# Score matmuls of the two heads of a pair issued alternately, in a two-layer hybrid attention trunk

## The chip, the cores and the metric

The kernel runs on one core of one Trainium2 chip. The metric is the time of one execution on the device, in microseconds (us); lower is better. The time before is 905.24 us, the median of 3 runs.

## What is computed

Two layers work on 256 tokens of width 1024, in float32. In each layer, the normalized input goes through one projection that gives q, k and v for 24 heads of 64 features and three gates. Twelve heads use softmax over dilated windows (three groups of four heads, mixed by their softmax sums), six use softmax with a block gate (at 256 tokens it is plain causal softmax, "MoBA"), and six use stick-breaking. The outputs are projected, gated, summed, projected again and added to the input; a squared-ReLU MLP follows. Shortened:

```python
for layer in range(2):
    h = rmsnorm(x, norm_mix)
    q, k, v, gates = split(h @ w_in)           # q and k of 18 heads with partial rotary
    o_a = dilated_mixture(q_a, k_a, v_a)       # 12 heads in 3 groups
    o_b = causal_softmax(q_b, k_b, v_b)        # 6 heads
    o_c = stick_breaking(q_c, k_c, v_c)        # 6 heads
    x = x + (g0 * (o_a @ wa) + g1 * (o_b @ wb) + g2 * (o_c @ wc)) @ w_o
    h = rmsnorm(x, norm_mlp)
    x = x + square(relu(h @ w_up)) @ w_down
out = rmsnorm(x, norm_final)
```

## The kernel before

All activations stay on the chip; 280 pieces of weights (128 x 1024 float32, 140 per layer) stream in from memory. Each piece is split into a high and a low part, `wh` on ACT (L115) and `wl` on DVE (L116), and a projection is three matmuls per 128 x 128 of weights: low part times high part of the input (L195), high times high (L196), high times low (L197), each with 256 columns.

In the first stage of a layer `MIX_ORDER` sets the order of the projections: v, then q and k of a pair of heads (`qk_pair`), then gates. After a pair's q and k the attention work that has become possible is put into the list `units`, and after each projection `run_units` takes one or two functions from its front. So attention work stands between projections. Behind that a scheduler orders the instructions of each engine by priority and by when their inputs should be there; what it made of the program is the order in which PE and the others execute.

One pair of heads shares a tile of q and k: head 0 lies on partitions 0 to 63, head 1 on 64 to 127. A score matmul contracts over 64 features and so uses only half of the array's rows: `scores` (L280) for softmax, `scores_t` (L284) for stick-breaking. They are plain float32, and each is recorded in the trace as two weight loads and two matmuls; the projections, in a rounded float32 format, are recorded as one of each.

- `att_softmax` with three groups (the dilated heads, twice per layer): its function `score` makes four units of scores, one after the other: head 0 and head 1 for the first 128 queries (3 x 128 columns each, in the two halves of the PSUM tile `s0`, a bank each), then head 0 and head 1 for the other queries (3 x 256 columns, a PSUM tile `s1` of two banks per head). After each comes `softmax_rows`: DVE adds the mask and finds the extreme (L311), ACT takes exp (L313), DVE normalizes (L315, L319).
- `att_softmax` with one group (MoBA, three times per layer): one PSUM tile, a bank per head, with 256 and 128 columns each.
- `att_c` (stick-breaking, three times per layer): `logs` writes the scores of both heads to one PSUM tile, a bank per head, and works them over with ACT, DVE, POOL and matmuls by a triangle (L415 to L418).
- `values` transposes the softmax rows on PE (L364 to L366) and multiplies with v (L306, L307).

PSUM tiles of the tag `s` have two buffers, shared by all of these. The scores of a head were written as

```python
for j in range(2):
    for g in range(3):
        scores(s0[:, j, g * P:(g + 1) * P], fs[g], j, T0, T0)
    softmax_rows(...)
```

Of the kernel before, what the change touches and what calls it, by code (L numbers as in the profile page):

```python
# [15 lines left out]
P = 128  # L16
D = 1024
KT = D // P
S = 256
# [39 lines left out]
def trunk(ctx: ExitStack, tc: tile.TileContext, w, x, norms, gfin, consts, out):  # L59
# [21 lines left out]
    def s_bank():  # L81
        return PS("s", [P, 2, 512], 2)
# [3 lines left out]

# [1 line left out]
    raw = {}  # L88
# [63 lines left out]
    def norm_split(hl, nrm, d):  # L152
        """high and low parts of x * g for one tile of features"""
        g = cst["norms"][:, nrm, d:d + 1]
        act.activation(hl[:, 0, d], xres[:, d], AF.Copy, scale=g)
        dve.scalar_tensor_tensor(hl[:, 1, d], xres[:, d], g, hl[:, 0, d].bitcast(F32),
                                 op0=ALU.mult, op1=ALU.subtract)

    def sumsq(d, acc):
        """acc += x*x over the tiles of features"""  # L160
        if d == 0:
            act.activation(acc, xres[:, d], AF.Square)
        else:
            sq = T("sq", [P, S], 3)
            act.activation(sq, xres[:, d], AF.Square)  # L165
            pool.tensor_tensor(acc, acc, sq, op=ALU.add)  # L166

    def rms_cols(acc):
        """[128, 2]: the factor of each token"""
        p = t_bank()  # L170
        for h in range(2):
            pe.matmul(p[:, h:h + 1], acc[:, h * P:(h + 1) * P], ones[:, 0:1], start=True, stop=True)
        r = T("rc", [P, 2], 8)
        dve.tensor_scalar(r, p[:, 0:2], 1.0 / D, EPS, op0=ALU.mult, op1=ALU.add)
        rc = T("rc", [P, 2], 8)
        pool.tensor_tensor(rc, r, mhalf, op=ALU.pow)
        return rc

    def bcast(rc):
        """PSUM [128, 256]: the factor of each token on every partition"""  # L180
        dg = T("sq", [P, 2, P], 3)
        for h in range(2):
            dve.tensor_scalar(dg[:, h], ident, rc[:, h:h + 1], None, op0=ALU.mult)
        p = t_bank()
        pe.matmul(p[:, 0:S], ones, dg.rearrange("p a b -> p (a b)"), start=True, stop=True)
        return p[:, 0:S]

    def proj(dst, n, hl, nk=KT, first=True, last=True, koff=0, woff=0):
        """dst[128 features, 256] (+)= W piece^T X"""
        hi, lo = split(n)  # L190
        for k in range(nk):
            c = (woff + k) * P
            a = (first and k == 0)
            z = (last and k == nk - 1)
            pe.matmul(dst, lo[:, c:c + P], hl[:, 0, koff + k], start=a, stop=False, skip_group_check=True)  # L195
            pe.matmul(dst, hi[:, c:c + P], hl[:, 0, koff + k], start=False, stop=False, skip_group_check=True)  # L196
            pe.matmul(dst, hi[:, c:c + P], hl[:, 1, koff + k], start=False, stop=z, skip_group_check=True)  # L197
# [12 lines left out]
    for layer in range(DEPTH):  # L210
# [9 lines left out]
        def normalized():  # L220
            """high and low parts of x * g * r"""
            for d in range(KT):
# [5 lines left out]

# [1 line left out]
        V = {}  # L230
# [26 lines left out]

# [1 line left out]
        QK = {}  # L259
# [30 lines left out]
        def o_head(po, oF, j):  # L290
            """o^T of a head: the parts from the high and the low part of v are added"""
            tmp = T("tmp", [DH, S], 2)
            act.activation(tmp, po[DH:P, 0:S], AF.Copy)
            dve.tensor_tensor(oF[j * DH:(j + 1) * DH], po[0:DH, 0:S], tmp, op=ALU.add)
# [5 lines left out]
        def pv_mm(po, head, kt, ph, pl, first, last):  # L300
            """po[v high and low, q] += v^T p^T"""
            c, s = divmod(head, 8)
# [18 lines left out]
        def att_softmax(fs, kt_out, units):  # L321
            """two heads (one pair) over the union of the keys of the groups fs"""
            G = len(fs)
            p0 = {}
            p1 = {}
            mA = cst["maskA"] if G == 3 else cst["maskB"].unsqueeze(1)

            def score():
                den = T("den", [P, 4], 3)
                if G == 3:  # L330
                    s0 = s_bank()
                    t0 = T("wk", [P, 2, 3, P], WK)
                    for j in range(2):
                        for g in range(3):
                            scores(s0[:, j, g * P:(g + 1) * P], fs[g], j, T0, T0)
                        softmax_rows(t0[:, j], s0[:, j, 0:384].rearrange("p (a b) -> p a b", a=3),
                                     mA[:, :, T1], den[:, j:j + 1])
                        p0[j] = t0[:, j]
                    for j in range(2):
                        s1 = s_bank()  # L340
                        t1 = T("wk", [P, 3, S], WK)
                        sf = s1.rearrange("p a b -> p (a b)")
                        for g in range(3):
                            scores(sf[:, g * S:(g + 1) * S], fs[g], j, T1, TT)
                        softmax_rows(t1, sf[:, 0:768].rearrange("p (a b) -> p a b", a=3), mA, den[:, 2 + j:3 + j])
                        p1[j] = t1
                else:
                    s1 = s_bank()
                    t1 = T("wk", [P, 2, 384], WK)
                    for j in range(2):  # L350
                        scores(s1[:, j, 0:S], fs[0], j, T1, TT)
                        scores(s1[:, j, S:384], fs[0], j, T0, T0)
                        softmax_rows(t1[:, j, 0:S], s1[:, j, 0:S], cst["maskB"], den[:, j:j + 1])
                        softmax_rows(t1[:, j, S:384], s1[:, j, S:384], cst["maskB"][:, T1], den[:, 2 + j:3 + j])
                        p1[j] = t1[:, j:j + 1, 0:S]
                        p0[j] = t1[:, j:j + 1, S:384]

# [19 lines left out]

            units += [score, lambda: values(0), lambda: values(1)]

        def att_c(i, units):  # L380
# [13 lines left out]
            def strict(x):  # L394
                """zero where the key isn't before the query"""
                for y in diag(x):
# [3 lines left out]
            def logs():  # L400
                st = s_bank()
                for j in range(2):
                    scores_t(st[:, j, 0:S], f, j, TT, T0, True)
                    scores_t(st[:, j, S:384], f, j, T1, T1, False)
                z = st[:, :, 0:384]
# [66 lines left out]

# [1 line left out]
        mg = hilo_slot()  # L474
# [14 lines left out]

# [1 line left out]
        acc = T("acc", [P, S], 1)  # L491
# [11 lines left out]

# [1 line left out]
        n = base + 76  # L505
# [228 lines left out]
```

## Time and profile before

| | |
|---|---|
| Median of 3 runs | 905.24 us (905.21 to 905.29) |
| Profiled execution, span from first to last instruction | 903.7 us |
| PE matmul busy | 891.9 us (99%), 6672 matmuls |
| DVE, ACT, POOL busy | 602.0, 493.8, 56.5 us (67%, 55%, 6%) |
| Granted TensorE clock | 0.9 or more of full speed in all 40 slices |
| Memory traffic | 151.5 MB, mean 168 GB/s |

The median lies 1.5 us above the span of the profiled execution. A matmul's recorded duration overlaps the next one's, so a busy PE does not mean that nothing is to be gained; what a matmul costs is read from the distance between the starts of neighbouring matmuls. The chain of waits is followed back from the last instruction and tells which engine's work the end hangs on.

### The profile page before, as it was taken

The page shows a single profiled execution, that of the slowest core. Times are in us where ns is not written, and L with a number is a line of the kernel's source. Part 1 is how long each engine was busy: PE and PEld are TensorE (multiplying, and loading weights), DVE is VectorE, ACT ScalarE, POOL GpSimd, SP SyncE. Part 2 cuts the span into 40 slices and gives each one's busy share as a digit, 9 for nine tenths or more (in the row PEclk, how much of TensorE's full clock was granted, in tenths as well). Part 3 has the DMA queues.
Part 4 walks back from the last instruction along what each step waited for, and adds up shares of the span by engine and source line. Part 5 has one row for each costly group of instructions (what it writes and reads, how often), then busy time and mean ns, then how long its engine had stood idle before and what let it go on. Part 6 is the DMA issues. An engine that isn't in the chain of part 4 may idle for free.

```text
span 903.7 us, 16383 instructions
## 1 busy us (share of the span) xinstructions
PE 891.9 (99%) x6672; PEld 846.8 (94%) x6672; DVE 602.0 (67%) x899; ACT 493.8 (55%) x724; POOL 56.5 (6%) x72
## 2 busy tenths in 40 slices
PE   8999999999999999999999999999999999999997
PEld 6899999999999999999988999999999999999995
DVE  6887777764986555555588868688558865555554
ACT  5655555667464444444466565656573654444442
POOL 7000100000020000000020101000000300000000
PEclk9999999999999999999999999999999999999999
DMA  8764434444656666666556544344456656566541
GB/s 301 234 189 136 142 118 139 128 153 156 182 157 201 193 182 181 182 182 184 164 186 188 171 134 139 119 140 123 157 164 187 187 171 201 187 186 188 185 140 46
DMA packets 43562, 151.47 MB, mean 168 GB/s; under 512 B 4960, under 2 KB 6368, under 8 KB 43488
## 3 DMA queue, kind: packets, MB, share of 16 engines
q1 hardware_dynamic: 43056, 149.90, 53.0%
q8 instruction: 52, 0.85, 0.4%
q10 hardware_dynamic: 432, 0.54, 0.2%
q14 instruction: 22, 0.18, 0.1%
HBM read 149.37 MB, written 1.05 MB: 166 GB/s over the span
## 4 chain that ended last, share of the span: by engine, by line
PE 91%; DVE 5%; DMA 2%; issue 1%; ACT 0%; SPq 0%; POOL 0%; POOLq 0%; DVEq 0%; ACTq 0%
PE mm L195 18%; PE mm L196 17%; PE mm L197 17%; PE s L546 3%; PE s L548 3%; PE s L547 3%; PE s L280 3%; PE s L572 3%; PE s L573 3%; PE s L574 3%; DVE wl L116 2%; DMA raw<-in_w_dram 2%; PE s L197 2%; PE s L196 2%; PE s L195 2%
## 5 line engine op out<-in xcount | busy, mean ns | idle before, releaser
L116 DVE TENSOR_TENSOR wl<-raw,wh 128x1024 fp32r<-128x1024 f32 (+1 forms) x282 | 345.1, 1226 | 227.1 <-ACT wh L115 226.9
L115 ACT ACTIVATE wh<-raw 128x1024 fp32r<-128x1024 f32 (+1 forms) x282 | 295.8, 1053 | 305.7 <-PE mm L197 175.5
L195 PE MATMUL mm<-hl,wl 128*128 128x256 f32 x1344 | 383.2, 285 | 1.7 <-DVE xres L496 1.7
L196 PE MATMUL mm<-hl,wh 128*128 128x256 f32 x1344 | 382.6, 285 | 0.0
L197 PE MATMUL mm<-hl,wh 128*128 128x256 f32 x1344 | 380.3, 284 | 0.2 <-DVE hl L227 0.2
L195 PEld LDWEIGHTS mm<-hl,wl 128*128 128x128 f32 x1344 | 256.9, 191 | 6.6 <-issue 2.7
L196 PEld LDWEIGHTS mm<-hl,wh 128*128 128x128 f32 x1344 | 257.0, 191 | 3.8 <-issue 2.0
L197 PEld LDWEIGHTS mm<-hl,wh 128*128 128x128 f32 x1344 | 256.3, 191 | 0.8 <-DVE hl L227 0.4
L546 PE MATMUL s<-ga,wl 128*128 128x256 f32 x256 | 72.5, 284 | 0.0
L547 PE MATMUL s<-ga,wh 128*128 128x256 f32 x256 | 72.3, 283 | 0.0
L548 PE MATMUL s<-ga,wh 128*128 128x256 f32 x256 | 72.2, 283 | 0.0
L572 PE MATMUL s<-wl,ga 128*128 128x512 f32 x128 | 50.1, 391 | 0.0
L573 PE MATMUL s<-wh,ga 128*128 128x512 f32 x128 | 50.0, 391 | 0.0
L546 PEld LDWEIGHTS s<-ga,wl 128*128 128x128 f32 x256 | 49.1, 192 | 0.5 <-DVE sq L633 0.2
L574 PE MATMUL s<-wh,ga 128*128 128x512 f32 x128 | 49.5, 389 | 0.0
L547 PEld LDWEIGHTS s<-ga,wh 128*128 128x128 f32 x256 | 49.1, 192 | 0.1
L548 PEld LDWEIGHTS s<-ga,wh 128*128 128x128 f32 x256 | 49.0, 192 | 0.2 <-DVE ga L535 0.2
L166 POOL TENSOR_TENSOR acc<-acc,sq 128x256 f32<-128x256 f32 x21 | 19.6, 934 | 414.0 <-ACT sq L165 239.6
L195 PE MATMUL s<-hl,wl 128*128 128x256 f32 x128 | 36.2, 283 | 0.0
L196 PE MATMUL s<-hl,wh 128*128 128x256 f32 x128 | 36.2, 283 | 0.0
L197 PE MATMUL s<-hl,wh 128*128 128x256 f32 x128 | 36.2, 283 | 0.0
L280 PE MATMUL s<-qk 64*128 64x128 f32 (+1 forms) x144 | 32.0, 347 | 0.0
(139 smaller groups left out, 1162.3 us busy)
## 6 DMA issues: line engine op xcount, KB each, us to landing
raw<-in_w_dram SPq DMA_DIRECT2D x278, 512.0 KB, 4.2
raw<-in_w_dram SPq DMA_DIRECT2D x4, 256.0 KB, 4.3
xres<-in_x_dram SPq DMA_DIRECT2D x8, 128.0 KB, 5.6
wk<-in_gfin_dram SPq DMA_DIRECT2D x2, 256.0 KB, 4.3
out_dram<-V SPq DMA_DIRECT2D x2, 256.0 KB, 2.3
out_dram<-V ACTq DMA_DIRECT2D x2, 256.0 KB, 2.2
c_maskA<-in_maskA_dram SPq DMA_DIRECT2D x1, 384.0 KB, 6.1
c_rope<-in_rope_dram SPq DMA_DIRECT2D x1, 256.0 KB, 5.6
```

Source lines behind the costliest of these rows:

```text
L115: act.activation(hi[:, c:c + step], r[:, c:c + step], AF.Copy)
L116: dve.tensor_tensor(lo[:, c:c + step], r[:, c:c + step], hi[:, c:c + step].bitcast(F32), op=ALU.subtract)
L195: pe.matmul(dst, lo[:, c:c + P], hl[:, 0, koff + k], start=a, stop=False, skip_group_check=True)
L196: pe.matmul(dst, hi[:, c:c + P], hl[:, 0, koff + k], start=False, stop=False, skip_group_check=True)
L197: pe.matmul(dst, hi[:, c:c + P], hl[:, 1, koff + k], start=False, stop=z, skip_group_check=True)
L280: pe.matmul(dst, t[own, 0, qs], t[own, 1, ks], start=True, stop=True, skip_group_check=True)
L546: pe.matmul(dst, lo[:, c], uh[:, j % 2], start=a, stop=False, skip_group_check=True)
L547: pe.matmul(dst, hi[:, c], uh[:, j % 2], start=False, stop=False, skip_group_check=True)
L548: pe.matmul(dst, hi[:, c], ul[:, j % 2], start=False, stop=z, skip_group_check=True)
L572: pe.matmul(dst, uh[:, j % 2, k], lo[:, c], start=j == 0, stop=False)
L573: pe.matmul(dst, uh[:, j % 2, k], hi[:, c], start=False, stop=False)
L574: pe.matmul(dst, ul[:, j % 2, k], hi[:, c], start=False, stop=j == 2 * npairs - 1)
```

## The change

Scores of the two heads of a pair are written alternately instead of one head after the other, in `att_softmax` and in `logs`. In `att_softmax` with three groups, the second half of the queries becomes a function of its own in the list of units, so that an entry more stands there per dilated pair, and it takes its two PSUM tiles before its first matmul. Both heads' scores are now written before the first `softmax_rows`.

```diff
+            def softmax_first():
+                s0 = s_bank()
+                t0 = T("wk", [P, 2, 3, P], WK)
+                for g in range(3):
+                    for j in range(2):
+                        scores(s0[:, j, g * P:(g + 1) * P], fs[g], j, T0, T0)
+                for j in range(2):
+                    softmax_rows(t0[:, j], ...)
+                    p0[j] = t0[:, j]
+            def softmax_second():
+                s1 = [s_bank().rearrange("p a b -> p (a b)") for _ in range(2)]
+                for g in range(3):
+                    for j in range(2):
+                        scores(s1[j][:, g * S:(g + 1) * S], fs[g], j, T1, TT)
+                for j in range(2):
+                    t1 = T("wk", [P, 3, S], WK)
+                    softmax_rows(t1, ...)
+                    p1[j] = t1
+            def softmax_one():
+                s1 = s_bank()
+                t1 = T("wk", [P, 2, 384], WK)
+                for j in range(2):
+                    scores(s1[:, j, 0:S], fs[0], j, T1, TT)
+                for j in range(2):
+                    scores(s1[:, j, S:384], fs[0], j, T0, T0)
+                for j in range(2):
...
             def score():
...
                 if G == 3:
...
-                    for j in range(2):
-                        for g in range(3):
-                            scores(s0[:, j, g * P:(g + 1) * P], fs[g], j, T0, T0)
-                        softmax_rows(t0[:, j], ...)
...
-                    for j in range(2):
-                        s1 = s_bank()
...
-                        for g in range(3):
-                            scores(sf[:, g * S:(g + 1) * S], fs[g], j, T1, TT)
-                        softmax_rows(t1, ...)
+                    softmax_first()
                 else:
...
+                    softmax_one()
...
-            units += [score, lambda: values(0), lambda: values(1)]
+            units += [score] + [softmax_second] * (G == 3) + [lambda: values(0), lambda: values(1)]
...
             def logs():
                 st = s_bank()
                 for j in range(2):
                     scores_t(st[:, j, 0:S], f, j, TT, T0, True)
+                for j in range(2):
                     scores_t(st[:, j, S:384], f, j, T1, T1, False)
```

Take a run of score matmuls with nothing between them for one block. Counted over the whole order of PE, there were 38 blocks before (32 of L280, 6 of L284), and there are 30 now (20 of L280, 10 of L284). The number of instructions is the same on every engine.

Three places of the first layer show it; the second layer has the same pattern. The names: `s` is a PSUM tile of scores, `qk` a pair's q and k, and the last number tells tiles apart.

First place, PE, the first dilated pair. The first fence is before (`s_137` holds the first queries of both heads, `s_143` the other queries of head 0, `s_147` those of head 1); "..." stands for other matmuls, mostly projections.

```order
L280 MATMUL s_137_781<-qk_110_620 128x128
L280 MATMUL s_137_781<-qk_124_706 128x128
...
L280 MATMUL s_143_801<-qk_110_620 128x256
L280 MATMUL s_143_801<-qk_124_706 128x256
...
L280 MATMUL s_137_781<-qk_133_773 128x128
L280 MATMUL s_143_801<-qk_133_773 128x256
...
L280 MATMUL s_147_812<-qk_110_620 128x256
L280 MATMUL s_147_812<-qk_124_706 128x256
L280 MATMUL s_147_812<-qk_133_773 128x256
```

The same pair now (`s_154` and `s_155` hold the other queries of head 0 and head 1; "x2" is one matmul of each head):

```order
L280 MATMUL s_137_781<-qk_110_620 128x128 x2
L280 MATMUL s_137_781<-qk_124_706 128x128 x2
...
L280 MATMUL s_137_781<-qk_133_773 128x128 x2
...
L280 MATMUL s_154_895<-qk_110_620 128x256
L280 MATMUL s_154_895<-qk_124_706 128x256
L280 MATMUL s_154_895<-qk_133_773 128x256
L280 MATMUL s_155_896<-qk_110_620 128x256
L280 MATMUL s_155_896<-qk_124_706 128x256
L280 MATMUL s_155_896<-qk_133_773 128x256
```

Five places became three (before, the three first-query matmuls of head 1 stood at a place of their own, between the third and the fourth shown). In the last one the scheduler put head 0's three matmuls ahead of head 1's; in the second dilated pair they alternate.

Second place, PE, the scores of a stick-breaking pair and of the first MoBA pair, before:

```order
L284 MATMUL s_192_1063<-qk_191_1060 128x256
L284 MATMUL s_192_1063<-qk_191_1060 128x128
...
L280 MATMUL s_321_1795<-qk_302_1700 128x256
L280 MATMUL s_321_1795<-qk_302_1700 128x128
```

and now:

```order
L284 MATMUL s_201_1130<-qk_180_1018 128x256 x2
L284 MATMUL s_201_1130<-qk_180_1018 128x128
L306 MATMUL t_162_917<-ph_167_934,V_51_266 128x256
L284 MATMUL s_201_1130<-qk_180_1018 128x128
...
L280 MATMUL s_332_1889<-qk_295_1664 128x256 x2
L280 MATMUL s_332_1889<-qk_295_1664 128x128 x2
```

Before, the two `L284` rows were followed at once by the same two for head 1, and the two `L280` rows of head 1 stood some 60 matmuls later. Now the MoBA pair is one run of four, and a matmul of `values` (L306) stands inside the stick-breaking pair's four.

Third place, DVE, the first dilated pair, now; `oF` belongs to the stick-breaking head whose values come just before, and `wl` are weight splits:

```order
L294 TENSOR_TENSOR oF_112_626<-t_115_635,tmp_116_640 64x256
L311 ISA wk_138_782,mn_139_789<-s_137_781,c_maskA_104 128x384
...
L311 ISA wk_138_782,mn_141_795<-s_137_781,c_maskA_104 128x384
...
L116 TENSOR_TENSOR wl_179_991<-raw_177_988,wh_178_990 128x1024
...
L311 ISA wk_156_903,mn_157_904<-s_154_895,c_maskA_104 128x768
...
L116 TENSOR_TENSOR wl_195_1067<-raw_193_1064,wh_194_1066 128x1024
L311 ISA wk_159_910,mn_160_911<-s_155_896,c_maskA_104 128x768
```

Before, weight splits stood between the `L311` of the four units; now the two of the first queries follow each other, and both heads' reads of the other queries stand around one split.

## Rows read from the trace of the kernel before

**Rows 1.** The page's head, busy times by engine, and granted clock in 40 slices

```profile
span 903.7 us, 16383 instructions
PE 891.9 (99%) x6672; PEld 846.8 (94%) x6672; DVE 602.0 (67%) x899; ACT 493.8 (55%) x724; POOL 56.5 (6%) x72
...
PEclk9999999999999999999999999999999999999999
...
PE 91%; DVE 5%; DMA 2%; issue 1%; ACT 0%; SPq 0%; POOL 0%; POOLq 0%; DVEq 0%; ACTq 0%
```

**Rows 2.** Busy time by stretch; this one holds layer 1's attention

```profile
core 0: us, PE busy (x) PEld busy (x) DVE busy (x) ACT busy (x) POOL busy (x), PEclk, DMA share, GB/s
55.00:204.00 149.00, 149.00 (x1192) 142.05 (x1191) 112.03 (x212) 87.69 (x151) 7.96 (x12) 1.00 0.44 138
```

**Rows 3.** The longest two of PE's five kinds of waits: us, times, longest

```profile
PE mm L195 <- DVE xres L496: 1.7, 2, 0.8
PE mm L245 <- DVE wl L116: 1.6, 3, 0.9
```

**Rows 4.** PE in time: two records of one head's scores, 128 columns (start, length, instruction)

```profile
170.85 0.28 PE L196 MATMUL mm<-hl,wh 128*128 128x256 f32 x1
170.97 0.28 PE L197 MATMUL mm<-hl,wh 128*128 128x256 f32 x1
171.18 0.48 PE L280 MATMUL s<-qk 64*128 64x128 f32 x2
171.60 0.39 PE L195 MATMUL mm<-hl,wl 128*128 128x256 f32 x1
171.82 0.28 PE L196 MATMUL mm<-hl,wh 128*128 128x256 f32 x1
```

**Rows 5.** The same: six records, 128 columns, one head

```profile
80.77 0.28 PE L197 MATMUL mm<-hl,wh 128*128 128x256 f32 x1
80.98 0.93 PE L280 MATMUL s<-qk 64*128 64x128 f32 x6
...
82.07 0.28 PE L196 MATMUL mm<-hl,wh 128*128 128x256 f32 x1
```

**Rows 6.** The same: six records, 256 columns, one head

```profile
85.29 0.28 PE L195 MATMUL mm<-hl,wl 128*128 128x256 f32 x1
85.50 1.56 PE L280 MATMUL s<-qk 64*128 64x256 f32 x6
...
87.21 0.28 PE L197 MATMUL mm<-hl,wh 128*128 128x256 f32 x1
```

**Rows 7.** PE in time: eight records of one head (four of 128, four of 256 columns)

```profile
113.00 1.57 PE L280 MATMUL s<-qk 64*128 64x128 f32 x8
114.50 0.38 PE L195 MATMUL mm<-hl,wl 128*128 128x256 f32 x1
```

**Rows 8.** The same: eight records of two heads, stick-breaking

```profile
55.13 0.28 PE L197 MATMUL mm<-hl,wh 128*128 128x256 f32 x1
55.34 0.93 PE L284 MATMUL s<-qk 64*128 64x256 f32 x8
56.20 0.39 PE L195 MATMUL mm<-hl,wl 128*128 128x256 f32 x1
56.42 0.28 PE L196 MATMUL mm<-hl,wh 128*128 128x256 f32 x1
```

**Rows 9.** Score matmuls by shape: records, busy us, mean ns, idle before

```profile
L280 PE MATMUL s<-qk 64*128 64x256 f32 x72 | 21.3, 402 | 0.0
L280 PE MATMUL s<-qk 64*128 64x128 f32 x72 | 13.3, 291 | 0.0
```

**Rows 10.** PE and then DVE in time, at the first dilated pair

```profile
77.07 0.92 PE L280 MATMUL s<-qk 64*128 64x128 f32 x4
...
78.28 0.42 DVE L294 TENSOR_TENSOR oF<-t,tmp 64x256 f32<-64x256 f32 x1
...
81.95 0.56 DVE L311 CUSTOM_DVE_ANT_1 wk<-s,c_maskA 128x384 f32<-128x384 f32 x1 [0.35 <-PE s L280]
```

More of the change, by code (lines that the diff above doesn't have):

```diff
@@ L325, in att_softmax @@
             p1 = {}
+            env = {}
             mA = cst["maskA"] if G == 3 else cst["maskB"].unsqueeze(1)
+            def softmax_first():
[5 more added lines that the diff above has]
+                for j in range(2):
+                    softmax_rows(t0[:, j], s0[:, j, 0:384].rearrange("p (a b) -> p a b", a=3),
+                                 mA[:, :, T1], env["den"][:, j:j + 1])
+                    p0[j] = t0[:, j]
@@ new lines, in softmax_second @@
+            def softmax_second():
[5 more added lines that the diff above has]
+                    t1 = T("wk", [P, 3, S], WK)
+                    softmax_rows(t1, s1[j][:, 0:768].rearrange("p (a b) -> p a b", a=3), mA, env["den"][:, 2 + j:3 + j])
+                    p1[j] = t1
@@ new lines, in softmax_one @@
+            def softmax_one():
[6 more added lines that the diff above has]
+                for j in range(2):
+                    softmax_rows(t1[:, j, 0:S], s1[:, j, 0:S], cst["maskB"], env["den"][:, j:j + 1])
+                    softmax_rows(t1[:, j, S:384], s1[:, j, S:384], cst["maskB"][:, T1], env["den"][:, 2 + j:3 + j])
+                    p1[j] = t1[:, j:j + 1, 0:S]
+                    p0[j] = t1[:, j:j + 1, S:384]
@@ L328, in score @@
             def score():
-                den = T("den", [P, 4], 3)
+                env["den"] = T("den", [P, 4], 3)
                 if G == 3:
-                    s0 = s_bank()
-                    t0 = T("wk", [P, 2, 3, P], WK)
-                    for j in range(2):
-                        for g in range(3):
-                            scores(s0[:, j, g * P:(g + 1) * P], fs[g], j, T0, T0)
-                        softmax_rows(t0[:, j], s0[:, j, 0:384].rearrange("p (a b) -> p a b", a=3),
-                                     mA[:, :, T1], den[:, j:j + 1])
-                        p0[j] = t0[:, j]
-                    for j in range(2):
-                        s1 = s_bank()
-                        t1 = T("wk", [P, 3, S], WK)
-                        sf = s1.rearrange("p a b -> p (a b)")
-                        for g in range(3):
-                            scores(sf[:, g * S:(g + 1) * S], fs[g], j, T1, TT)
-                        softmax_rows(t1, sf[:, 0:768].rearrange("p (a b) -> p a b", a=3), mA, den[:, 2 + j:3 + j])
-                        p1[j] = t1
-                else:
[L348 to L356, printed above, removed]
```

## The prediction

> **What bounds the kernel now.** I read the page's head first: PE is busy for 891.9 of 903.7 us, the chain that ended last is 91% PE, and the granted clock stands at its upper level, 2.4 GHz, in every slice [rows 1]. The reader is to see there that only PE's own time counts. Then the stretches: in layer 1's attention, 55 to 204 us, PE is busy without a gap, while DVE has 112.0 us of work in 149 (75%), ACT 87.7 (59%) and DMA a share of 0.44 [rows 2]. Third, PE's waits: five kinds in the whole profile, the longest two 1.7 and 1.6 us, the others on L130, L245 and L197, none before a score matmul, a transposition or a value matmul [rows 3]. So the 38 blocks of score matmuls lie on the path, and what a block costs PE is what the kernel pays.
>
> **What a block costs.** Busy time doesn't tell it, since neighbours overlap; I take starts. Projections start 0.12 us apart (170.85, 170.97) [rows 4]. I measure a block from the last projection before it to the second one behind it, and take off two such steps, 0.24:
> - two records of 128 columns (one matmul): 170.97 to 171.82 is 0.85, leaves 0.61 [rows 4];
> - six such records: 80.77 to 82.07 is 1.30, leaves 1.06 [rows 5]. The difference of 0.45 for four records makes 0.112 us each, so 0.61 holds 0.22 of work and 0.38 of going over to half the array's rows and back;
> - six records of 256 columns: 85.29 to 87.21 is 1.92, less 0.24 and 0.38 leaves 1.30, or 0.216 us each [rows 6].
>
> One rule follows: 0.38 us per block, 0.224 per matmul of 128 columns and 0.432 per matmul of 256, when all are of one head.
>
> With two heads it is otherwise. Eight records of one head, four of each width, need 1.50 us to the next projection (113.00 to 114.50) [rows 7]; the same eight, half of them of each head, need 0.86 (55.34 to 56.20) [rows 8]. By the rule the one-head block is 0.38 + 1.31. The two-head block from 55.13 to 56.42 is 1.29, less 0.24 and 0.38 leaves 0.67, half of 1.31. So the two halves of the array work at the same time, and a block costs what its longer head costs. The order of the program at that place was head 0, head 0, head 1, head 1, as in the second place shown: the pairing needs the heads side by side, and alternation within a block was not needed.
>
> **The sum.** Before, no L280 block holds both heads. There are 72 records of each width, hence 36 matmuls of each [rows 9]: 36 x 0.224 + 36 x 0.432 = 23.6 us, and 32 blocks x 0.38 = 12.2: 35.8. The six stick-breaking blocks are paired already: 6 x (0.38 + 0.66) = 6.2. Together 42.0 us.
>
> Now, per layer, by the longer head: the first queries of the first dilated pair are two blocks, 0.45 + 0.22, those of the second pair three, 0.22 + 0.45 + 0.22 (a matmul of head 0 is split off there); the other queries are two blocks of 1.30, if the three-and-three one pairs too; MoBA has three of 0.66. That makes 6.1 us in ten blocks; two layers: 12.3 + 20 x 0.38 = 19.9. Stick-breaking gets worse: in four of six pairs the last matmul of head 1 is cut off by a value matmul and pays a block of its own, 0.38 + 0.22 = 0.61, so 6.2 + 2.4 = 8.6. Together 28.5 us. The gain is 42.0 - 28.5 = 13.5 us: 12 fewer L280 blocks give 4.6, pairing 11.3, and the stick-breaking cuts take back 2.4.
>
> The transposes and value matmuls are as many as before and stand differently among the projections; their rows give a change of a few tenths at most. I take 0.3 us off the gain for this and for small waits: it lies between nothing, since PE waits for no engine in the attention stretch before [rows 3], and the waits of the second rival.
>
> The DMA and the weight splits are not edited. Per layer some 6.6 us go from PE's time in the stretch, so DVE comes to 112 in 142 us (79%) and ACT to 62%: both still have room, and their work is what the same wait for PE set free before. If that cover were gone, wl would be late first, since each projection waits for it.
>
> Against its own time: 903.7 - 13.2 = 890.5 of span; the median stands 1.5 us above the span of the profiled execution, which the change doesn't touch: 905.2 - 13.2 = **892.0 us**.
>
> **The rivals.**
> 1. *Three and three don't pair.* In one block per layer head 0's three matmuls of 256 columns stand ahead of head 1's. If PE could not start head 1 before head 0's sixth record, the block would be five records of 0.216 = 1.08 us longer, 2.2 in all: 894.2. For it: the only two-head blocks in the trace have two matmuls per head ahead of the other's. Against it: there head 1 is not held up by head 0's later records, for 0.67 us leaves no room for that [rows 8].
> The Trainium skill, TensorE: Matmul & The Clock Gate, Part 3 (The mechanism), has a rule that would make this the case: matmuls start and end in program order, and weight loads alone are pulled ahead. This trace speaks against the rule: by it head 1's first record at the stick-breaking block could not have started before head 0's fourth, 0.54 us in, and the 0.86 us would have been 1.40.
> 2. *New waits eat a part.* Both heads' softmax comes at once, and the second queries take both PSUM buffers. At the first dilated pair head 1's tile needs both reads of the first queries done. Before, the values' last DVE step began 1.21 us after the score block's start (77.07 to 78.28) and took 0.42; two reads of 0.56 and their short ends then finish near 2.9 us [rows 10]. PE comes there after 0.6 of block and 26 projections (3.1): 3.7. So 0.8 us of cover, and less than a weight split's length would remove it. At ten softmax pairs, 0.2 to 0.9 us each makes 894 to 901. Against it: the scheduler set the order so that inputs should be there, and before it kept PE free of waits.
> 3. *Slower than before.* The same place, with a weight split or a late ACT step ahead of the reads: PE waits in order, the projections behind it stand still, the splits they would have released come late, and the next block finds DVE late again. This costs more than the 13.5 gained from a mean wait of 1.35 us at each of the ten pairs; with 2 us, 912. In its favour only that DVE is the busiest engine beside PE; against it that 25% of DVE is free [rows 2].
> 4. *L280 doesn't pair as L284 does.* Then only the 4.6 of blocks less 2.4 and 0.3 is left: 903.3. Heads lie on the same halves of the array and in different PSUM banks in both, so I see no reason.
>
> **How the numbers follow.** Forecast, all pairs and nearly no waits, 890.5 to 893.5: 0.73. First rival 0.08, second 0.12, third 0.03, fourth 0.04. Low end: 905.2 - 13.5 and 1.2 more, should the cuts in stick-breaking cost only half: 890.5. High end: into the second rival with the first inside, 896.5. Outside lie most of the fourth and third, a part of the second and the forecast's edges, 0.2 together. About 0.2% (1.8 us) is what a measurement of this kernel can tell from no change. Faster 0.95 (forecast, first, second, half of the fourth), same 0.02, slower 0.03.
>
> **What would show it.** Right: paired L280 blocks with eight records take 0.86 us to the next start and six-and-six blocks about 1.5, not 2.8; 30 blocks; PE's matmuls of the attention stretch end some 6.6 us earlier per layer; no wait on a line of softmax or values. Wrong: a block of twelve records near 2.6 us (first rival), idle time before L280 or the transposes with DVE as releaser (second and third), eight records at 1.5 us (fourth). Over 896.5 the idle rows must say where; under 890.5 the price of a block is not what I read.

## The result and the profile after

The changed kernel takes 893.44 us (median of 4 runs, 893.42 to 894.52) against 905.23 us in the same comparison (905.17 to 905.29): a ratio of 0.9872, interval 0.986 to 0.9885, or 11.8 us less. Forecast were 892.0 us in a range of 890.5 to 896.5. The profiled execution has a span of 891.4 us and took 893.46 us as a whole.

The page's head of the changed kernel, and the stretch of layer 1's attention (start and end of the stretch, its length, then busy us and records of PE, PEld, DVE, ACT and POOL, granted clock, DMA share, GB/s):

```profile
span 891.4 us, 16382 instructions
PE 878.8 (99%) x6672; PEld 837.8 (94%) x6672; DVE 602.4 (68%) x899; ACT 491.7 (55%) x724; POOL 52.4 (6%) x72
PEclk9999999999999999999999999999999999999999
PE 94%; DVE 3%; issue 1%; DMA 1%; ACT 0%; SPq 0%; POOLq 0%; DVEq 0%; ACTq 0%
...
55.00:197.00 142.00, 142.00 (x1185) 137.39 (x1185) 110.52 (x209) 85.63 (x148) 5.51 (x12) 1.00 0.48 145
```

Against [rows 1, 2] one thing has changed: PE's busy time is 13.1 us less with the same 6672 matmuls. The granted clock is at 2.4 GHz all through, as before; DVE, ACT and the DMA do about the same work in a stretch that is shorter. PE is still busy without a gap there, and PE still makes up the chain that ended last.

The score matmuls by shape (records, busy us, mean ns of one, idle before):

```profile
L280 PE MATMUL s<-qk 64*128 64x256 f32 x72 | 11.6, 405 | 0.0
L280 PE MATMUL s<-qk 64*128 64x128 f32 x72 | 8.1, 297 | 0.0
```

The mean duration of one record is what it was (405 and 297 ns; 402 and 291 in [rows 9]), but the 256-column records of L280 cover 11.6 us instead of 21.3, and those of 128 columns 8.1 instead of 13.3. The records now lie over each other in time, two by two. Busy time can't price that, since a record also overlaps its neighbours of the projections; the chain that ended last lists PE's time piece by piece (start, us, what), and there each block of scores is one piece:

```profile
55.34 0.85 PE s L284 x8
...
80.04 2.03 PE s L280 x12
94.80 0.85 PE s L284 x6
...
123.83 1.50 PE s L280 x12
...
158.19 0.85 PE s L280 x8
```

Four of the five are as forecast: eight records of two heads 0.85 us (stick-breaking and MoBA), the six that are left of a cut stick-breaking pair also 0.85, and twelve records in alternating order 1.50. The twelve records in the order three and three took 2.03: neither the 1.50 of full pairing nor the 2.58 of none (1.50 and the 1.08 of the first rival). That is the first surprise.

The second is at the end of the stage, in the output projections of layer 1 (timeline of all engines; a bracket gives idle time before and its releaser):

```profile
224.08 0.28 PE L197 MATMUL s<-hl,wh 128*128 128x256 f32 x1
...
224.35 0.19 PEld L195 LDWEIGHTS s<-hl,wl 128*128 128x128 f32 x1 [0.19 <-DVE wk L499]
224.35 0.39 PE L195 MATMUL s<-hl,wl 128*128 128x256 f32 x1
...
224.57 0.28 PE L196 MATMUL s<-hl,wh 128*128 128x256 f32 x1
```

Neighbouring projections are 0.12 us apart, but here the steps are 0.27 and 0.22: PE loses 0.25 us, and again at 663.56 in layer 2. No such wait stood in the profile before. DVE and ACT show where it comes from:

```profile
211.37 5.25 ACT L483 ACTIVATE ga<-ga 128x768 f32<-128x768 f32 x7
216.52 1.99 ACT L115 ACTIVATE wh<-raw 128x1024 fp32r<-128x1024 f32 x2
```

```profile
217.60 2.36 DVE L116 TENSOR_TENSOR wl<-raw,wh 128x1024 fp32r<-128x1024 f32 x2 [7.08 <-ACT wh L115]
219.87 0.95 DVE L499 TENSOR_TENSOR wk<-s,ga 128x768 f32<-128x768 f32 x1
...
223.35 0.95 DVE L499 TENSOR_TENSOR wk<-s,ga 128x768 f32<-128x768 f32 x1
```

ACT takes the sigmoids of the gates as soon as the last exp is done, now seven in a row (six before, from 213.87 to 218.4). Behind them the weight splits `wh` wait, DVE stands idle for 7.08 us (6.15 before) and then has the overdue low parts `wl` and the gate products (L499) to do together. The second product ends at 224.30, and the fourth output projection, which needs that product's PSUM tile and would have begun at 224.20, waits for it.

PE's other waits are of the kinds that it had before [rows 3], all on projections and on L130 (the longest four of six kinds: us, times, longest):

```profile
PE mm L195 <- DVE xres L511: 1.4, 2, 0.8
PE mm L245 <- DVE wl L116: 1.4, 3, 0.9
PE mm L245 <- ACT wh L115: 1.2, 1, 1.2
PE t L130 <- POOL mhalf L144: 1.1, 1, 1.1
```

The wait in the output projections is not in this list: a matmul's record is 0.28 us long where the next starts after 0.12, so PE's rows cover a wait of up to 0.16 us, and only the weight load (PEld) shows it.

One stretch of each layer shows where the 11.8 us came from: the one from the first L284 record to the first record of the second output projection. In layer 1 it took 169.43 us before (55.34 to 224.77) and takes 163.17 now (55.27 to 218.44), 6.26 less; in layer 2 it is 6.27 less. These 12.5 us are all of the gain; the sigmoid wait behind it gives 0.5 back.

### The profile page after: what moved, and what is told of

Its sections match the earlier page's. It is cut to its first block, busy times and chain, and to the rows that moved or that the text cites. A ratio compares the mean times of both kernels' runs of the same rounds, so it can differ in the third digit from the quotient of the medians.

```text
span 891.4 us, 16382 instructions
## 1 busy us (share of the span) xinstructions
PE 878.8 (99%) x6672; PEld 837.8 (94%) x6672; DVE 602.4 (68%) x899; ACT 491.7 (55%) x724; POOL 52.4 (6%) x72
## 4 chain that ended last, share of the span: by engine, by line
PE 94%; DVE 3%; issue 1%; DMA 1%; ACT 0%; SPq 0%; POOLq 0%; DVEq 0%; ACTq 0%
PE mm L195 18%; PE mm L197 18%; PE mm L196 18%; PE s L561 3%; PE s L563 3%; PE s L562 3%; PE s L587 3%; PE s L588 3%; PE s L589 3%; PE s L280 2%; PE s L195 2%; PE s L197 2%; PE s L196 2%; PE s L245 2%; DVE wl L116 2%; PE s L247 2%
## 5 line engine op out<-in xcount | busy, mean ns | idle before, releaser
L587 PEld LDWEIGHTS s<-wl,ga 128*128 128x128 f32 x128 | 24.1, 188 | 5.0 <-DVE V L622 0.4
```

The source lines that it names most:

```text
L587: pe.matmul(dst, uh[:, j % 2, k], lo[:, c], start=j == 0, stop=False)
```

## The experiments

**The theory.** A block pays 0.38 us for going to half the array's rows and back, plus the longer head's records. Heads in one block run side by side if they are near enough in PE's order, alternating or not. How near is shown by the block of three and three, record by record (a matmul makes two records, so each head has six). Up to 80.505 us and then from 80.50 to 80.51 there run on PE:

```profile
79.97 0.91 PE L280 MATMUL s<-qk 64*128 64x256 f32 x3
80.29 0.70 PE L280 MATMUL s<-qk 64*128 64x256 f32 x3
```

In the trace head 0's first three records start at 79.966, 80.286 and 80.502, head 1's first at 80.507, 5 ns behind head 0's third, with three of head 0's records not yet started. So I take it that PE starts a record when at most three records of the other head ahead of it have not started; I call this a reach of three.

**The rivals.** That it is the alternation itself that pairs heads; that the gain comes from the softmax units, which are cut and spaced otherwise; and for the three-and-three block, that PE takes records in order and something else made it 0.55 us shorter than that.

The three runs that come first change before or take back parts of the change. The edits:

```diff
 logs_only: the kernel before, with
                 for j in range(2):
                     scores_t(st[:, j, 0:S], f, j, TT, T0, True)
+                for j in range(2):
                     scores_t(st[:, j, S:384], f, j, T1, T1, False)
 moba_only: the kernel before, one group only, with
                     for j in range(2):
                         scores(s1[:, j, 0:S], fs[0], j, T1, TT)
+                    for j in range(2):
                         scores(s1[:, j, S:384], fs[0], j, T0, T0)
+                    for j in range(2):
                         softmax_rows(...)
 dil_only: the changed kernel, with both of these places as before
```

### Alternation alone, in stick-breaking

> The kernel before with one edit: the stick-breaking scores are written alternately. Price-of-blocks theory (0.38 us per block, plus 0.112 us per record of 128 columns and 0.216 per record of 256, by the longer head): the order on PE still has 38 blocks with the same heads in each, 42.1 us before and with the edit, and these six blocks were paired already: 905.2 us, within 0.5. Rival, alternation itself matters: pairing would get better or worse in six blocks of 1.04 us, so up to 2 us either way.

Measured: 905.29 us, ratio 0.9997 (0.9988 to 1.0006). The first such block in PE's timeline:

```profile
55.12 0.92 PE L284 MATMUL s<-qk 64*128 64x256 f32 x8
55.98 0.39 PE L195 MATMUL mm<-hl,wl 128*128 128x256 f32 x1
```

It is 0.86 us, as long as with head 0, head 0, head 1, head 1 [rows 8]. Where heads are already side by side, alternation is worth nothing.

### The MoBA pairs alone

> The kernel before with one edit: the MoBA pairs' scores are written for both heads, and then both heads' softmax. The order on PE has 36 blocks instead of 38, and most MoBA matmuls of the two heads now share a block: by the price of blocks 37.9 us instead of 42.1, so 4.3 us less, 901.0 us. Rival, the softmax of both heads at once makes PE wait: at six pairs 0.3 to 0.7 us each would give most of it back, 903 to 905, with idle time before the transposes.

Measured: 900.53 us, ratio 0.9947 (0.9934 to 0.9961). The scheduler leaves only one of the three pairs of a layer in one block (three of the other blocks hold both heads too, with one matmul of each), so that blocks fall from 38 to 36 and no further. The whole one needs 0.85 us, all four matmuls of both heads:

```profile
162.69 0.92 PE L280 MATMUL s<-qk 64*128 64x256 f32 x8
163.54 0.39 PE L195 MATMUL mm<-hl,wl 128*128 128x256 f32 x1
```

The price of the blocks gives 4.3 us, the measurement 4.7 to 5.0, by which run of the kernel before it is set against.

### The dilated pairs alone

> The changed kernel with the MoBA and the stick-breaking scores written as before: only the dilated pairs alternate, and their second queries are a unit of their own. 34 blocks, 34.0 us by the longer head and 34.9 to 35.1 if the two three-and-three blocks are held up as in the changed kernel: 7.0 to 7.2 us less than before, 898.1 us. With the MoBA part alone that would account for 11.4 of the 11.8 us of the whole change. Rival, the gain is from the new unit's place in the order and not from pairing: then this kernel has nearly the whole 11.8, 893.5.

Measured: 898.95 us, ratio 0.9928 (0.9914 to 0.9942), with 34 blocks; the block of three and three is again 2.03 us long. This part gives 6.3 to 6.6 us, and with the MoBA part's 4.7 to 5.0 that is nearly all of 11.8.

### No unit of its own for the other queries

```diff
                     softmax_first()
+                    softmax_second()
...
-            units += [score] + [softmax_second] * (G == 3) + [...]
+            units += [score] + [...]
```

> The changed kernel with the second queries of the dilated pairs in the same unit as the first ones again; scores still alternate. The order on PE has 34 blocks and the two heads' matmuls of the second queries fall apart into blocks of one head: 34.4 us by the price of blocks against 29.4 to 29.7 in the changed kernel, so 4.7 to 5.0 us slower than it, 898.3 us. Rival, the separate unit is not needed for the gain: 893.4.

Measured: 897.02 us, ratio 0.9907 (0.9893 to 0.992): 3.6 us slower than the changed kernel. Without its own unit, the scheduler breaks up the other queries' scores into pieces of one head each, which pair with nothing:

```profile
70.83 1.13 PE L280 MATMUL s<-qk 64*128 64x256 f32 x4
71.89 0.39 PE L195 MATMUL mm<-hl,wl 128*128 128x256 f32 x1
```

These four records of head 0 alone take 1.06 us; by the rule the same time would have done for four of head 1 beside them. So the rival of the units is right in this: the unit is worth something, because it decides which matmuls come to stand together. By the price of its 34 blocks this run should stand at 897.5; it is 0.5 to 0.8 us better, and I don't know why.

### The other queries alternating by force

```diff
+                mm = None
                 for g in range(3):
                     for j in range(2):
-                        scores(...)
+                        with (tc.issue_after(mm.ins) if mm else nullcontext()):
+                            mm = scores(...)
```

> The changed kernel with one edit: the six matmuls of the second queries are chained in the order they are written in, so that the first dilated pair alternates too instead of three and three. Theory, PE starts a record at most three records ahead of the other head's waiting ones: the two three-and-three blocks (2.03 us to the next start) become like the alternating ones (1.50), 1.07 us less: 892.4 us. Rival, the 0.53 us in these blocks were a wait for head 1's PSUM buffer: then the alternating block waits too, before its second record, and the time stays at 893.4.

Measured: 892.30 us (892.27 to 892.49), ratio 0.9856 (0.9839 to 0.9872). The block that was 2.03 long:

```profile
79.65 1.57 PE L280 MATMUL s<-qk 64*128 64x256 f32 x12
81.14 0.38 PE L195 MATMUL mm<-hl,wl 128*128 128x256 f32 x1
```

Now it is 1.49 (79.65 to 81.14), 0.54 less; twice that is 1.07 us, and the median is 1.14 lower than that of the changed kernel. In this trace head 1's first record starts 6 ns behind head 0's first, so it did not wait for its PSUM tile, and the rival falls. The scheduler's order of these two blocks cost what the reach of three says.

### No alternation anywhere

Every inner loop goes back to head 0 and then head 1; the units and the order of scores before softmax stay as changed.

```diff
-                for g in range(3):
-                    for j in range(2):
+                for j in range(2):
+                    for g in range(3):
                         scores(...)
```

> The changed kernel with no alternation anywhere: in each block head 0's matmuls are written before head 1's, with both heads' softmax behind them and the separate unit kept. The order on PE has 36 blocks, since the scheduler cuts the heads apart at the dilated pairs, and keeps two heads together in the MoBA and stick-breaking blocks. By the price of blocks 37.4 us against 29.4 to 29.7 in the changed kernel: 7.7 to 8.0 us slower, 901.3 us; the MoBA blocks of two and two take 0.86 us to the next start as the alternating ones do. Rival, alternation within a block is what pairs the heads: the MoBA blocks take 1.5 us, and the time is 905 or more.

Measured: 901.11 us, ratio 0.9954 (0.9939 to 0.9969). Two blocks show both sides:

```profile
161.45 0.93 PE L280 MATMUL s<-qk 64*128 64x256 f32 x8
162.31 0.39 PE L195 MATMUL mm<-hl,wl 128*128 128x256 f32 x1
```

```profile
79.95 1.56 PE L280 MATMUL s<-qk 64*128 64x256 f32 x6
81.44 0.38 PE L195 MATMUL mm<-hl,wl 128*128 128x256 f32 x1
```

The MoBA pair, two and two, takes 0.86 without alternation. Against the changed kernel 7.7 us are lost, by the price 6.6 of them in the other queries of the dilated heads: written head by head, most come out in blocks of one head, 1.49 us for three matmuls. So alternation in the source has a use after all, through the scheduler, in whose final order both heads' scores then stand together. That this comes from their priorities is my reading; no run shows it.

### Six and six

The second queries' scores are written twice over, head 0's six and then head 1's six, with the same result: this adds twelve score matmuls per layer that the kernel doesn't need.

```diff
-                for g in range(3):
-                    for j in range(2):
+                for j in range(2):
+                    for g in [0, 1, 2, 0, 1, 2]:
                         scores(...)
```

> The changed kernel with the second queries' scores of the dilated pairs written twice over, all six of head 0 before the six of head 1 (the same values are written to the same place again). It measures how far PE reaches past waiting records of the other head. If at most three waiting records can be passed: head 1's first record starts about 1.84 us after head 0's first (behind head 0's ninth record), the block of 24 records takes 4.6 us to the next start. If the reach is half of the other head's records, 1.2 us. If head 1 waited for a PSUM buffer in the changed kernel and there is no limit: 0.5 us as there. If in strict order: 2.5 us.

Measured in one run: 902.44 us, span 900.4. The block:

```profile
79.61 4.69 PE L280 MATMUL s<-qk 64*128 64x256 f32 x24
84.23 0.33 PE L378 MATMUL t<-c_ident,wk 128*128 128x128 f32 x1
```

and what runs on PE in its short stretch from 81.40 to 81.46:

```profile
81.23 0.70 PE L280 MATMUL s<-qk 64*128 64x256 f32 x3
```

The three records that run there end at 81.93; the last of them, head 1's first, is 0.48 long, as the first record of a head is, and so began at 81.45: 1.84 us into the block, 6 ns behind head 0's ninth record of twelve, with three not yet started. The block is 4.62 long. A start in order would have come with head 0's twelfth record, near 2.5, and a block of free pairing would be about 2.8 long. The reach of three holds in a block where it was forecast. Both blocks that show it have records of 256 columns, so three records are here also 768 columns, or 0.65 us of head 0's work: which of these PE goes by, no run tells apart.

### What the changed kernel leaves

Now the first queries of a dilated pair are chained into one block, the other queries right behind them, and the stick-breaking scores get a higher priority so that no value matmul cuts them. (`env` carries the last score matmul over, and `scores` now returns its matmul, as it does where the alternation is forced.)

```diff
-                for g in range(3):
+                mm = None
+                for g in (2, 0, 1):
                     for j in range(2):
-                        scores(s0[...], ...)
+                        with (tc.issue_after(mm.ins) if mm else nullcontext()):
+                            mm = scores(s0[...], ...)
+                env["mm"] = mm
...
-                    for j in range(2):
-                        scores(s1[j][...], ...)
+                    for j in (1, 0):
+                        with (tc.issue_after(mm.ins) if mm else nullcontext()):
+                            mm = scores(s1[j][...], ...)
...
+                with tc.high_priority(offset=300):
                     scores_t(...)
```

> The changed kernel with the order of the score matmuls held together: first queries start with the pair's tile that comes last, so that they form one block, second queries are chained behind them, and the stick-breaking scores have a higher priority so that no value matmul cuts them. 24 blocks, 26.7 us by the price of blocks against 29.4 to 29.7 in the changed kernel: 2.8 to 3.0 us less, 890.5 us. Rival, waits at the softmax come up when the scores stand closer: 892 to 895, with idle time of PE in the attention stretch.

Measured: 890.74 us (890.63 to 891.35), ratio 0.984 (0.9825 to 0.9855), with 24 blocks. One matmul of 256 columns of each dilated pair still stands by itself. PE's list of waits and that of its weight loads name no engine before a score, transposition or value matmul, so the rival did not come. The lost 0.25 us in the output projections is still there:

```profile
222.40 0.28 PE L197 MATMUL s<-hl,wh 128*128 128x256 f32 x1
222.67 0.39 PE L195 MATMUL s<-hl,wl 128*128 128x256 f32 x1
```

### The gate sigmoids spread out

On top of that kernel, four sigmoids stay up front, and the other four are issued each behind the ACT half of a weight split (kept in `wins`) in the loop of the output projections. The table load that follows the last sigmoid moves along with it.

```diff
-            for d in range(KT):
+            for d in range(3):
                 s = act.activation(G[d], G[d], AF.Sigmoid)
...
         for d in range(KT):
             n = base + 60 + d
+            if d + 3 < KT:
+                with tc.issue_after((wins[base + 62 + d] if d else s).ins):
+                    s = act.activation(G[d + 3], G[d + 3], AF.Sigmoid)
...
```

> The kernel of the run rest_cut with one more edit: the gate sigmoids on ACT no longer stand in one run of seven ahead of the weight splits; four come first, and the others one by one between the splits. Theory: in the changed kernel and in rest_cut the splits that wait behind the seven make DVE idle for 7.1 us, and the products with the gates come late, so that PE waits 0.25 us at the fourth out-projection of each layer (0.15 and 0.10 over the usual steps). Without it 0.5 us less than rest_cut: 890.2 us, and no step over 0.23 us between out-projections. Rival, these steps are not from the sigmoids: they stay, 890.7 us.

Measured: 890.16 us (889.91 to 891.09), ratio 0.9833 (0.9818 to 0.9847), the fastest of all. ACT, then DVE's longest wait of the profile (total, times, longest), then PE at the same place:

```profile
212.80 0.83 ACT L497 ACTIVATE ga<-ga 128x768 f32<-128x768 f32 x1
213.53 1.04 ACT L116 ACTIVATE wh<-raw 128x1024 fp32r<-128x1024 f32 x1
```

```profile
DVE wl L117 <- ACT wh L116: 216.9, 172, 4.9
```

```profile
222.45 0.28 PE L197 MATMUL s<-hl,wh 128*128 128x256 f32 x1
222.57 0.28 PE L198 MATMUL s<-hl,wh 128*128 128x256 f32 x1
222.69 0.28 PE L196 MATMUL s<-hl,wl 128*128 128x256 f32 x1
```

A sigmoid and a split alternate, DVE never waits longer than 4.9 us, and the steps here are 0.12 again in both layers. (The longest step that the trace still has in the output projections is 0.17, once per layer in the first of them, and the changed kernel has it too.) So the cause of the wait is shown. That the time follows is not shown by these two runs: 0.58 us less in the median than the kernel without this edit lies inside the two intervals, and the profiled spans (889.0 and 888.7) don't show it, because in the first 50 us PE waited 3.1 us for splits of weights and input (L246 and L198) in the one profile and 1.5 in the other.

### The changed kernel once more, beside it

> The changed kernel once more, on the same chip as gates_between: 893.4 us, as a measure for differences of less than 1 us between runs of different calls; the time around the profiled span 2.0 us again, if the 0.5 us more than in the first profile of before are the kernel's and not the profile's.

Measured: 893.47 us (893.4 to 893.52), ratio 0.9867 (0.9851 to 0.9884); its profiled execution took 893.52 us at a span of 891.5. That is 2.0 us around the span, but it is nothing peculiar to the changed kernel: the seven executions of the kernel before in this comparison have 1.75 to 2.06 us around spans of 903.0 to 903.9. So the 0.5 us were the first profile's. On one chip the version above is 3.3 us faster than the changed kernel.

### Price and measurement, all runs

The price is 0.38 us per block and the longer head's records with a reach of three, set against before's 42.1 us; measured is the median against the kernel before of the same comparison.

| run | blocks | by the price, us | measured, us |
|---|---|---|---|
| logs_only | 38 | 0.0 | -0.2 |
| moba_only | 36 | -4.3 | -5.0 |
| adjacent | 36 | -4.7 | -4.0 |
| dil_only | 34 | -7.2 | -6.6 |
| one_unit | 34 | -7.7 | -8.5 |
| the changed kernel, twice | 30 | -12.7 | -11.8, -12.1 |
| alt_forced | 30 | -13.5 | -12.8 |
| rest_cut | 24 | -15.4 | -14.4 |
| gates_between (the price has no term for its sigmoids) | 24 | -15.4 | -15.5 |

The ten comparisons follow the price within 1.1 us. For a block of three and three the price counts a delay of two records, 0.43 us; with the measured 0.54 the changed kernel stands at -12.4 and dil_only at -7.0.

The deviations have both signs, and the sign goes with the sigmoid wait. The traces of dil_only, adjacent, the changed kernel (both), alt_forced and rest_cut have the step of 0.27 us at the fourth output projection of each layer, and these gain 0.6 to 1.0 us less than the price. Those of logs_only, moba_only, one_unit and gates_between don't have it, and these gain 0.1 to 0.8 more. The wait makes up 0.5 us of this difference; what makes up the rest is open.

## Why the prediction was right, and where it was not

1. *What bounds the kernel.* Right: PE's busy time fell by 13.1 us, and the span went with it, by 12.3.
2. *The price of a block.* Right, and it held in blocks that the kernel before didn't have: 0.85 us for eight paired records, 1.50 for six and six alternating. A cut stick-breaking pair was priced as a block of 0.38 + 0.66 and one of 0.61:

```profile
94.52 0.28 PE L197 MATMUL mm<-hl,wh 128*128 128x256 f32 x1
94.73 0.92 PE L284 MATMUL s<-qk 64*128 64x256 f32 x6
95.57 0.39 PE L306 MATMUL t<-ph,V 128*128 128x256 f32 x1
95.89 0.48 PE L284 MATMUL s<-qk 64*128 64x128 f32 x2
...
96.53 0.28 PE L196 MATMUL mm<-hl,wh 128*128 128x256 f32 x1
```

From 94.52 to 96.53 is 2.01; less three steps of 0.12 for the other matmuls that leaves 1.65, the sum of the two.

The prediction laid the 0.38 us to half the rows without a look at another difference: the scores are plain float32 and the projections around them are not. The kernel before has a place that tells the two apart, a plain float32 matmul on all 128 rows between projections:

```profile
279.38 0.28 PE L195 MATMUL mm<-hl,wl 128*128 128x256 f32 x1
279.50 0.59 PE L185 MATMUL t<-sq,ones 128*128 128x256 f32 x2
...
280.05 0.28 PE L197 MATMUL mm<-hl,wh 128*128 128x256 f32 x1
```

From 279.38 to 280.05 is 0.67, less two steps 0.43: two records of 0.216 and nothing more. The 0.38 us go with the half rows.

3. *The step that failed: "two blocks of 1.30, if the three-and-three one pairs too".* In each layer one of the two is 0.54 us longer, because head 1's first record started only behind head 0's third. The first rival had named the place and the wrong alternative: it allowed only all or nothing, 0 or 1.08 us, and half came. The reason given against the rival was that at the stick-breaking block head 1 isn't held up by head 0's later records. True, but there just three of them stood in the way, so the row could not tell "any number" from "three". The sum with the measured size is 13.5 - 1.07 = 12.43 us, and the attention stretches gave 12.53.

The Trainium skill, TensorE: Matmul & The Clock Gate, Part 3 (The mechanism), says that matmuls start in program order. By it head 1's first record would have started with the last of head 0's, at about 0.65, 1.18 and 2.48 us into blocks with four, six and twelve records ahead (0.32 us from the first record to the second as in the block above, then 0.216 or 0.112 each). The measured starts are 0.014, 0.541 and 1.837 us (the prediction put the first in-order start at 0.54, as it counted 0.216 for the first record too): the measurement decides, and for records on the other half of the rows the order holds only beyond three.

4. *The small things.* The 0.3 us taken off in the attention stretch was not needed: the stretches fell by the price of the blocks. PE's list of waits and that of its weight loads name no engine before a score, transposition or value matmul, so the second and third rivals did not come at their place. A wait did come elsewhere, 0.25 us per layer in the output projections. I had looked for what DVE and ACT would be late with inside the stretch, and not at the run of sigmoids that stands at its end: seven sigmoids take ACT 5.25 us in the changed kernel and in rest_cut alike. From their end to PE's second output projection there were 6.4 us before (218.4 to 224.77), and now there are 1.8 (216.6 to 218.44).
5. *The time around the span.* The prediction set before's median beside the span of another execution and took 1.5 us. The 29 executions of the kernel before whose own span is on record beside the experiments have 1.7 to 2.1 us around spans of 902.6 to 904.1, and the changed kernel has 2.0 to 2.1. So the profile of 903.7 us was taken in a slightly long execution, and of the 1.4 us by which the median missed nothing has to be laid to this. The terms make it up: 13.5 us of gain, less 1.07 for the blocks of three and three and 0.5 for the sigmoids, is 11.9, and 11.8 were measured. Without the 0.3 us that were taken off for another reason, the forecast would have missed by 1.7.
6. *Rivals.* The first came in half; the second in another place and for 0.5 us; the third and the fourth did not come: every L280 block with both heads near each other is paired.

## What to carry to other kernels

Matmuls that use half the array's rows cost what their blocks cost: count the places where PE goes over to them, and in each block the longer half, not the records. To pair two halves, bring their matmuls into one uninterrupted run and within three records of each other (measured with records of 256 columns), and read the scheduler's final order, for source order and final order differ. When the engine that bounds gets faster by several us, look at the next long fixed run on another engine (here sigmoids in front of weight splits), because the first new wait may appear there.

## What the runs showed of the hardware beyond this

- A matmul on one half of the rows starts past waiting matmuls of the other half, but past at most three records: 14 ns, 0.541 us and 1.837 us into blocks with four, six and twelve of them ahead. The second and third have records of 256 columns alone, so that three records, 768 columns and 0.65 us of work can't be told apart; other shapes were not tried.
- Going over to half the rows and back took 0.38 to 0.39 us in 186 of the 204 blocks between projections in the traces of all kernels, and 0.44 to 0.47 in the others. Beside transposes and value matmuls, whose own steps are not all 0.12, the same count gives 0.19 to 0.49. A plain float32 matmul on all rows pays nothing of the kind (two records took 0.43 us). The Trainium skill, TensorEngine Tiling (Array Packing), Key Properties, has it that a change of tiling mode drains the array. That agrees with the 0.38 us, whose size is this case's; no run shows the draining itself.
- Paired records run at full speed on both halves: twelve alternating records of 256 columns take 1.50 us where six of one head alone take 1.49.
